# Raw projection tiles as fillers, finished at the merge, and first tiles multiplied as the input arrives

## The chip, the cores and the metric

One core of a Trainium2 chip runs the whole layer. The metric is the device time of one execution in microseconds, as a median of several runs. The engines are named as the profile names them: PE (TensorE, matmuls), PEld (its weight loads), DVE (VectorE), ACT (ScalarE), POOL (GpSimd) and SP (SyncE, which issues all DMAs of this kernel).

## The reference

A decoder layer over 1024 positions of width 1024. One projection of the normalized input feeds three mixers in parallel; their outputs are gated, merged and followed by a feed-forward part:

```python
proj = rmsnorm(x, g_mix) @ w_in
y_fox = forgetting_attention(fq, fk, fv, fox_f, ...)        # 8 heads of 64
y_sc = sb * causal_dwconv(sc * sv, sc_conv_w)               # 3 taps
dn_qkv = silu(causal_dwconv(dn_qkv, dn_conv_w))             # 4 taps
o_dn = gated_delta_rule(l2norm(dq), l2norm(dk_), dv_, g, beta)
y_dn = rmsnorm(o_dn, dn_norm_gain) * silu(z)
gates = sigmoid(br_gate)                                    # 3 x 1024 channels
merged = sum((ys @ w_branch) * gates)                       # over the 3 branches
x = x + merged @ w_o
x = x + (silu(u_gate) * u_val) @ w_down                     # u = dwconv3(rmsnorm(x) @ w_up)
x = x + sigmoid(rmsnorm(x, g_ple) @ w_ple_gate) * (p @ w_ple)
```

## The kernel before

Everything lies with channels on the 128 partitions and positions along the free axis. Each float32 operand is split into a high and a low float32r part, and a product takes three matmuls (high times high, high times low, low times high). A "tile" of the projection is 128 output channels: `dense` (line 151) makes it in two halves of 512 positions, each 8 input blocks times 3 matmuls into one PSUM bank, 48 matmuls in all, and hands each half to an evacuation function. `wload` (147) loads the 512 KB of weights and `wsplit` (139) splits them: ACT copies the high part, and POOL (in the merge and later DVE, line 949) subtracts to get the low part. The projection's operand is the unnormalized x; the factor 1/rms per position (`rs`) comes in as a product at each evacuation.

The input is read in `first_norm` (321): per block of 128 channels a DMA, the split into high and low (`norm_operand`, lines 267 and 268), squares on ACT and their sums (`sumsq`, line 277) on DVE for one half and on POOL for the other; 32 narrow matmuls for the few scalar logits stand after that, and `make_rstd` (280) gives `rs`. One tile, the first attention q, has its weights loaded early. `scalars` (383) works out decays and cumulative sums in a long series of small DVE instructions.

Then come three stages. The attention (lines 898 to 922) runs 8 heads in 4 blocks each (`softmax`, `weigh`), with q, k and v tiles of head pairs (`fox_proj`, 506). The solve (`dn_solve`, 720) inverts 32 triangular blocks: it builds the matrices (715, 731), transposes them on DVE (737), runs a substitution of 31 steps on DVE (743, 745), and joins blocks by small matmuls. The recursion (lines 932 to 946) steps a state through 8 chunks. All are chains on DVE and ACT, and between them `filler` (887) puts independent projection tiles by the table `PLAN` (31): letters k, v, q are DeltaNet tiles (`dn_tile`, 693: scaling at line 700, four taps at 470 and 472, silu at 666 to 674), s a tile of the short convolution (`short_conv`, 476: C, v and B of a channel block in turn), z an output gate (`z_tile`, 685), g a branch gate (`gate_tile`, 677). Each evacuation finishes its tile: scale, convolve, sigmoid, store. A filler may not be issued before a mark some steps back. The order on every engine is set by the framework's planner from simulated times, in program order of priority. During these stages two PSUM banks (`mm`) serve the tiles.

The merge (lines 958 to 1046) first makes the gate tiles that are left, 17 of 24, with six banks; then it multiplies each branch's output with its weights and the stored gates, in the order short convolution, attention, DeltaNet (its z product on POOL, line 984), and goes through w_o. The feed-forward stages follow and are not touched.

Of the kernel before, what the change touches and what calls it, by code (L numbers as in the profile page):

```python
# [7 lines left out]
F32 = mybir.dt.float32  # L8
# [40 lines left out]
def hybrid_block(ctx: ExitStack, tc: tile.TileContext, I, out, dbg=None):  # L49
# [254 lines left out]
    zdr = dr.tile([P, 4, T], F32, tag="zdr", name="zdr")  # L304
# [14 lines left out]
    early = {}  # L319

    def first_norm():
# [10 lines left out]
        xr, xg = [pt("xr", 8, T) for _ in range(KT)], []  # L332
# [9 lines left out]
        few = [smb(), smb()]  # L342
        for nb in range(2):
            for kt in range(KT):
                h, l = xg[kt]
                for n, x in ((32, h), (16, l)) if kt == 0 else ((16, l), (32, h)):
                    mm(few[nb][:n], wsp[:, kt * 32 : kt * 32 + n], x[:, NB[nb]], kt == 0 and n == 32,
                       kt == KT - 1 and n == 32)
        for kt in range(KT):
            sumsq(acc, xr[kt], kt == 0, (V, G))  # L350
        return xg, make_rstd(acc), few
# [124 lines left out]
    def short_conv(j):  # L476
        hold = {}

        def ev_sc(nb, ps):
            t = pt("sc", 3)  # L480
            V.tensor_tensor(out=t, in0=ps, in1=rs[:, NB[nb]], op=ALU.mult)
            hold["c", nb] = t

        def ev_sv(nb, ps):
            cv = conv_in(nb, hold.get(("cv", 0)), 3)
            hold["cv", nb] = cv
            t = cv[:, 2:514]
            V.tensor_tensor(out=t, in0=ps, in1=rs[:, NB[nb]], op=ALU.mult)
            G.tensor_tensor(out=t, in0=t, in1=hold["c", nb], op=ALU.mult)
            o = conv_out(cv, C_SC + 3 * j, 3)  # L490
            y = hold["c", nb]
            G.tensor_tensor(out=y, in0=o, in1=rs[:, NB[nb]], op=ALU.mult)
            hold["y", nb] = y

        def ev_sb(nb, ps):
            y = hold["y", nb]
            V.tensor_tensor(out=y, in0=ps, in1=y, op=ALU.mult)
            Q.dma_start(ydr[1][j][:, NB[nb]], y)

        def run(kind):  # L500
            u, f = {"c": (U_SC, ev_sc), "v": (U_SV, ev_sv), "b": (U_SB, ev_sb)}[kind]
            dense(wload(I["win"][u + j]), KT, xg, f)
        return run


    def fox_proj(j):
# [42 lines left out]
        def run(kind):  # L549
# [5 lines left out]
            dense(early.pop(u + j, None) or wload(I["win"][u + j]), KT, xg, f)  # L555
# [121 lines left out]
    def gate_tile(b, dt):  # L677
        def f(nb, ps):
            g = tmp("o")
            V.tensor_tensor(out=g, in0=ps, in1=rs[:, NB[nb]], op=ALU.mult)  # L680
            Q.dma_start(gdr[b, dt][:, NB[nb]], sigmoid(g))
        gdr[b, dt] = dr.tile([P, T], F32, tag=f"g{b}{dt}", name=f"g{b}{dt}")
        dense(wload(I["win"][U_GT + 8 * b + dt]), KT, xg, f)

    def z_tile(h):
        def f(nb, ps):
            z = tmp("o")
            V.tensor_tensor(out=z, in0=ps, in1=rs[:, NB[nb]], op=ALU.mult)
            silu(z)
            Q.dma_start(zdr[:, h, NB[nb]], z)  # L690
        dense(wload(I["win"][U_Z + h]), KT, xg, f)

# [27 lines left out]
    def dn_solve():  # L720
        A, TT = (pt(n, 1, 4096).rearrange("p (x j) -> p x j", j=P) for n in ("A", "TT"))
        G.memset(TT, 0.0)
# [517 lines left out]
```

## Time and profile before

| | us |
| --- | --- |
| median of 3 runs | 2048.36 (2048.19 to 2049.76) |
| the profiled execution | 2044.89 |
| span from its first to its last instruction | 2043.1 |

The profile is of one execution. Its page gives busy times of each engine and the costliest groups of instructions, and the trace can be asked for stretches, timelines, and who waited for whom. PE is the busiest engine. A busy time of PE says that matmuls were in flight, not at which rate; the rate is seen by their number in a stretch. The granted clock is a share of 2.4 GHz, and 0.5 of it is the lower level, 1.2 GHz. Idle time is put down to the instruction that ended it.

### The profile page before, as it was taken

What the parts mean: (1) busy time and instruction counts of PE and PEld (TensorE: products, weight loads), DVE (VectorE), ACT (ScalarE), POOL (GpSimd) and SP (SyncE); (2) the same over time, 40 slices, a digit from 0 to 9 for tenths busy, and PEclk for the clock granted to TensorE, in tenths of its full rate; (3) what the DMA queues carried; (4) which work ended last, traced back from release to release, by engine and by line L of the source; (5) the groups of instructions that cost most, each with busy time, mean ns of one, the idle gap of its engine ahead of it and who ended that gap; (6) DMA issues with size and microseconds to landing.
All of it is one profiled execution on the core that took longest, in us unless ns stands there. A gap on an engine that the chain in (4) does not pass through costs nothing. (4 is left out here: it accounts for less than half of the span.)

```text
span 2043.1 us, 25369 instructions
## 1 busy us (share of the span) xinstructions
PE 1959.1 (96%) x9281; PEld 1617.9 (79%) x9281; DVE 1368.0 (67%) x2190; ACT 903.1 (44%) x1639; POOL 575.5 (28%) x457
## 2 busy tenths in 40 slices
PE   6899999998987999999999999999999999999998
PEld 4788888887766888888888888777777777888887
DVE  7887888797999354222264636978787878544564
ACT  6566777765334334322221325544444444212351
POOL 4455335333444221000015310334343341000210
PEclk8999999999988999999999999999999999999999
DMA  3122121123311333522274523111222216432132
GB/s 147 56 73 77 45 69 55 61 69 88 106 70 49 108 105 92 191 98 103 95 273 154 184 99 134 62 52 64 91 83 73 92 63 227 144 93 73 52 108 89
DMA packets 96877, 202.63 MB, mean 99 GB/s; under 512 B 8720, under 2 KB 39792, under 8 KB 96752
## 3 DMA queue, kind: packets, MB, share of 16 engines
q1 hardware_dynamic: 96752, 201.01, 29.3%
q8 instruction: 73, 1.20, 0.2%
q14 instruction: 52, 0.43, 0.1%
HBM read 150.59 MB, written 50.38 MB: 98 GB/s over the span
## 5 line engine op out<-in xcount | busy, mean ns | idle before, releaser
L126 PE MATMUL mm<-xg,wo 128*128 128x512 f32 x6224 | 1508.5, 395 | 41.0 <-DVE cv L700 18.8
L126 PEld LDWEIGHTS mm<-xg,wo 128*128 128x128 f32 x6224 | 1166.8, 189 | 295.6 <-DVE wo L130 18.3
L126 PE MATMUL mm<-a,wo 128*128 128x512 f32 x1216 | 303.3, 389 | 0.0
L129 ACT ACTIVATE wo<-wr 128x512 fp32r<-128x512 f32 x232 | 144.6, 627 | 310.2 <-PE mm L126 301.9
L126 PEld LDWEIGHTS mm<-a,wo 128*128 128x128 f32 x1216 | 228.4, 188 | 47.9 <-ACT u L224 0.4
L130 POOL TENSOR_TENSOR wo<-wr,wo 128x512 fp32r<-128x512 f32 x94 | 131.6, 1405 | 173.0 <-ACT wo L129 149.7
L130 DVE TENSOR_TENSOR wo<-wr,wo 128x512 fp32r<-128x512 f32 x138 | 109.6, 794 | 61.6 <-ACT wo L129 60.8
L1141 DVE TENSOR_TENSOR a<-mm,a 128x512 f32<-128x512 f32 x96 | 65.2, 687 | 92.1 <-PE mm L126 92.0
L277 POOL TENSOR_TENSOR tmp<-tmp,tmp 128x512 f32<-128x512 f32 x21 | 27.7, 1324 | 286.9 <-ACT tmp L275 284.9
L472 DVE SCALAR_TENSOR_TENSOR o<-cv,cols,o 128x512 f32<-128x512 f32 x88 | 86.1, 984 | 6.2 <-ACT o L470 5.4
L970 DVE TENSOR_TENSOR tmp<-mm,rs 128x512 f32<-128x512 f32 x34 | 23.5, 691 | 91.2 <-PE mm L126 91.2
L130 DVE TENSOR_TENSOR wo<-wq,wo 128x512 fp32r<-128x512 f32 x68 | 79.1, 1165 | 2.9 <-ACT wo L129 2.7
L1054 DVE SCALAR_TENSOR_TENSOR o<-cw,cols,o 128x1024 f32<-128x1024 f32 x44 | 77.7, 1767 | 0.0
L984 POOL TENSOR_TENSOR yr<-yr,yr 128x1024 f32<-128x1024 f32 x4 | 9.6, 2397 | 240.6 <-DVE xg L130 211.8
L129 ACT ACTIVATE wo<-ws 128x512 fp32r<-128x512 f32 x80 | 50.2, 630 | 56.5 <-PE mm L126 56.4
L594 ACT ACTIVATE pp<-pp,small 128x512 f32<-128x512 f32 (+2 forms) x96 | 58.3, 610 | 28.7 <-DVE small L588 28.4
L674 POOL TENSOR_TENSOR o<-o,sg 128x512 f32<-128x512 f32 x32 | 46.5, 1453 | 74.1 <-ACT sg L669 64.9
L1086 POOL TENSOR_TENSOR cg<-o,cg 128x1024 f32<-128x1024 f32 x22 | 55.5, 2523 | 40.7 <-ACT cg L1085 40.7
L196 POOL TENSOR_TENSOR ws<-wq 128x512 f32<-128x512 f32 x20 | 29.3, 1466 | 109.8 <-DMA wq<-wup 109.8
L1002 POOL TENSOR_TENSOR a<-a,sg 128x512 f32<-128x512 f32 x32 | 50.6, 1584 | 32.4 <-DVE sg L1001 32.4
L196 POOL TENSOR_TENSOR ws<-wq,wq 128x512 f32<-128x512 f32 x20 | 43.7, 2184 | 56.3 <-DVE wo L130 52.3
L1052 ACT ACTIVATE o<-cw,cols 128x1024 f32<-128x1024 f32 x22 | 25.4, 1157 | 75.3 <-DVE cw L220 75.3
(287 smaller groups left out, 2496.1 us busy)
## 6 DMA issues: line engine op xcount, KB each, us to landing
wr<-win SPq DMA_DIRECT2D x64, 512.0 KB, 3.5
wq<-wup SPq DMA_DIRECT2D x44, 512.0 KB, 3.6
sg<-g SPq DMA_DIRECT2D x48, 256.0 KB, 3.1
ad<-o SPq DMA_DIRECT2D x20, 512.0 KB, 3.8
wq<-ad SPq DMA_DIRECT2D x20, 512.0 KB, 4.6
wr<-wdn SPq DMA_DIRECT2D x20, 512.0 KB, 3.7
g<-tmp SPq DMA_DIRECT2D x34, 256.0 KB, 2.0
wr<-wbr SPq DMA_DIRECT2D x12, 512.0 KB, 3.6
```

Of the source, the lines that this page charges most:

```text
L126: pe[0] = nc.tensor.matmul(o, lhsT=l, rhs=r, start=start, stop=stop, skip_group_check=more)
L129: S.activation(h, x, AF.Copy)
L130: (eng or V).tensor_tensor(out=l, in0=x, in1=h.bitcast(F32), op=ALU.subtract)
L196: (G if e == "g" else V).tensor_tensor(out=o, in0=x, in1=y, op=op)
L277: eng[nb].tensor_tensor(out=acc[nb], in0=acc[nb], in1=sq, op=ALU.add)
L472: V.scalar_tensor_tensor(out=o, in0=cv[:, i : i + 512], scalar=col(c0 + i), in1=o, op0=ALU.mult, op1=ALU.add)
L594: S.activation(t[:, :w], t[:, :w], AF.Exp, bias=mn[:, k - 1 : k], scale=-1.0, accum_out=sm[:, i : i + 1])
L674: G.tensor_tensor(out=o, in0=o, in1=sg, op=ALU.mult)
L1002: G.tensor_tensor(out=m, in0=m, in1=t, op=ALU.add)
L1054: V.scalar_tensor_tensor(out=o, in0=cv[:, i : i + T], scalar=col(c0 + i), in1=o, op0=ALU.mult, op1=ALU.add)
L1086: G.tensor_tensor(out=sg, in0=o, in1=sg, op=ALU.mult)
L1141: V.tensor_tensor(out=x2[dt][:, NB[nb]], in0=ps, in1=x2[dt][:, NB[nb]], op=ALU.add)
```

## The change

Fillers of the kinds s, z and g become one kind, r: a raw tile, copied out of its bank by ACT and stored unscaled (24 of them: 12 of the short convolution, 4 output gates, 8 branch gates). What their evacuations did (scale by rs, convolve, sigmoid, multiply) is done at the merge, one item after each of the 16 gate tiles that are left there, on DVE and ACT from loaded raw tiles. The DeltaNet tiles all move ahead of the solve; the solve has eight raw tiles, the recursion's first six steps the last nine. In `first_norm` each arriving block is at once multiplied for the scalar logits, for the first q tile and for one raw tile (in banks of its own, five of `sm` where there were four); the sums of squares and these two tiles' weight splits are all on DVE. q and k of the first heads come ahead of `scalars`. The branches are merged in the order 0, 1, 2, the zeroing of TT is cut in eight, and one evacuation takes another buffer.

```diff
-PLAN = {"start": "kgs", "tail": "", "solve": "zzzzzvvvv",
-        "steps": ["zs", "sz", "zs", "s", "s", "ks", "g", "sgs", "gs"],
-        "fox": [["", "", "", "s"],
-                ["k", "gs", "", ""],
-                ["", "", "", ""],
+PLAN = {"start": "krr", "tail": "", "solve": "rrrrrrrr",
+        "steps": ["rr", "rr", "rr", "r", "r", "r", "r", "r", "r"],
+        "fox": [["", "", "", "v"],
+                ["k", "v", "", ""],
+                ["", "", "", "r"],
                 ["", "v", "", ""],
-                ["ks", "", "k", "k"],
-                ["", "", "g", ""],
-                ["", "", "", "s"],
-                ["v", "s", "g", ""]]}
+                ["kr", "", "q", "v"],
+                ["", "", "q", "r"],
+                ["", "", "", "q"],
+                ["k", "q", "r", ""]]}
...
         for kt in range(KT):
             Q.dma_start(xr[kt], I["xT"][kt])
             xg.append(norm_operand(kt, xr[kt], C_G1))
-            if kt == 1:
-                early[U_FQ] = wload(I["win"][U_FQ])
+            if kt == 0:
+                wq = wload(I["win"][U_FQ], eng=V)
+            if kt == 2:
+                wr, _, _, evac = raw_tile(spare["r"].pop(0), V)
+            if kt:
+                sumsq(acc, xr[kt - 1], kt == 1, (V, V))
+        sumsq(acc, xr[KT - 1], False, (V, V))
+        for kt in range(KT):
+            for nb in range(2):
+                h, l = xg[kt]
...
+            for w, ps in ((wq, pq), (wr, pr_)):
+                for nb in range(2):
+                    step(ps[nb], w, kt, xg[kt], nb, kt == 0, kt == KT - 1)
+        for nb in range(2):
+            evac(nb, pr_[nb])
...
+    def raw_tile(u, eng=None):
+
+        raw[u] = dr.tile([P, T], F32, tag=f"r{u}", name=f"r{u}")
+
+        def f(nb, ps):
+            o = tmp("o")
+            S.activation(o, ps, AF.Copy)
+            Q.dma_start(raw[u][:, NB[nb]], o)
+        return wload(I["win"][u], eng=eng), KT, xg, f
...
+            def short_conv(j):
+                c, v, cv = load(raw[U_SC + j]), load(raw[U_SV + j]), yr(T + 2)
+                V.memset(cv[:, 0:2], 0.0)
+                t = cv[:, 2 : T + 2]
+                mul(t, c, v)
+                mul(t, t, rs)
+                mul(t, t, rs)
+                S.activation(c, cv[:, 0:T], AF.Copy, scale=col(C_SC + 3 * j))
+                for i in (1, 2):
+                    V.scalar_tensor_tensor(out=c, in0=cv[:, i : i + T], scalar=col(C_SC + 3 * j + i), in1=c,
+                                           op0=ALU.mult, op1=ALU.add)
+                b = load(raw[U_SB + j])
+                mul(c, c, b)
+                mul(c, c, rs)
+                Q.dma_start(ydr[1][j], c)
+
+            def dn_gated(j):
+                z, y, sg = load(raw[U_Z + j]), load(ydn[:, j, :]), yr()
+                mul(z, z, rs)
+                S.activation(sg, z, AF.Sigmoid)
+                mul(z, z, sg)
+                mul(y, y, z)
+                Q.dma_start(ydr[2][j], y)
+
+            def gate(b, dt, nb, ps):
+                g = tmp()
+                if ps is None:
+                    Q.dma_start(g, raw[U_GT + 8 * b + dt][:, NB[nb]])
+                mul(g, g if ps is None else ps, rs[:, NB[nb]])
+                S.activation(g, g, AF.Sigmoid)
+                Q.dma_start(gdr[b, dt][:, NB[nb]], g)
...
+                    if u not in raw:
+                        dense(wload(I["win"][u]), KT, xg, lambda nb, ps, b=b, dt=dt: gate(b, dt, nb, ps))
+                        if rest:
+                            rest.pop(0)()
```

## Rows read from the trace of the kernel before

**Rows 1.** The page, part 1: busy time, share of the span and number of instructions of each engine.

```profile
PE 1959.1 (96%) x9281; PEld 1617.9 (79%) x9281; DVE 1368.0 (67%) x2190; ACT 903.1 (44%) x1639; POOL 575.5 (28%) x457
```

**Rows 2.** The stretches view, 50 us each: length, then busy time and number of instructions of PE, PEld, DVE, ACT and POOL, the granted TensorE clock as a share of 2.4 GHz, the busy share of the DMA engines and GB/s.

```profile
0.00:50.00 50.00, 33.87 (x119) 20.84 (x120) 36.55 (x42) 29.91 (x52) 23.63 (x21) 0.86 0.40 150
50.00:100.00 50.00, 44.66 (x191) 35.83 (x189) 44.03 (x85) 28.17 (x51) 21.11 (x17) 0.93 0.16 54
...
450.00:500.00 50.00, 43.29 (x234) 36.38 (x233) 35.83 (x95) 26.38 (x61) 13.41 (x14) 0.93 0.24 72
500.00:550.00 50.00, 47.33 (x237) 39.07 (x235) 44.80 (x101) 21.41 (x36) 21.11 (x16) 1.00 0.48 138
550.00:600.00 50.00, 40.28 (x153) 31.41 (x154) 49.69 (x61) 17.40 (x29) 21.41 (x17) 0.90 0.17 61
600.00:650.00 50.00, 38.62 (x201) 32.23 (x199) 48.57 (x72) 19.20 (x33) 22.21 (x20) 0.90 0.15 53
650.00:700.00 50.00, 44.91 (x363) 40.42 (x362) 23.16 (x40) 16.98 (x37) 14.22 (x11) 0.97 0.34 96
...
850.00:900.00 50.00, 50.00 (x222) 41.42 (x221) 11.66 (x17) 11.12 (x18) 0.00 (x0) 1.00 0.38 134
...
1700.00:1750.00 50.00, 49.26 (x216) 40.03 (x215) 40.03 (x50) 18.90 (x24) 3.40 (x2) 1.00 0.79 285
```

**Rows 3.** The same view of three longer stretches: the attention, the triangular solve, and the recursion.

```profile
100.00:470.00 370.00, 364.75 (x1893) 306.04 (x1894) 307.69 (x720) 265.25 (x561) 163.73 (x136) 1.00 0.20 65
...
490.00:650.00 160.00, 136.24 (x634) 111.04 (x633) 147.37 (x243) 59.02 (x99) 65.49 (x55) 0.94 0.28 86
...
675.00:850.00 175.00, 171.19 (x1012) 149.44 (x1012) 78.41 (x198) 69.19 (x174) 36.90 (x32) 1.00 0.40 123
```

**Rows 4.** Timelines of the first 100 us, of PE, then DVE, ACT and POOL: start, duration (both us), engine, line, operation, output<-input, how many in a row, and in brackets the idle time before the first with what ended it.

```profile
6.76 2.10 PE L126 MATMUL sm<-xg,wsp 128*32 128x512 f32 x4 [6.76 <-ACT xg L267]
...
11.49 1.59 PE L126 MATMUL mm<-xg,wo 128*128 128x512 f32 x4
...
14.48 2.92 PE L126 MATMUL mm<-xg,wo 128*128 128x512 f32 x12
...
72.40 8.11 PE L126 MATMUL mm<-xg,wo 128*128 128x512 f32 x24 [4.49 <-DVE o L540]
...
6.74 1.41 DVE L268 SCALAR_TENSOR_TENSOR xg<-xr,cols,xg 128x512 fp32r<-128x512 f32 x2 [2.91 <-ACT xg L267]
...
12.31 3.33 DVE L268 SCALAR_TENSOR_TENSOR xg<-xr,cols,xg 128x512 fp32r<-128x512 f32 x2 [1.29 <-ACT xg L267]
15.57 3.50 DVE L277 TENSOR_TENSOR acc<-acc,tmp 128x512 f32<-128x512 f32 x2
...
31.68 1.48 DVE L277 TENSOR_TENSOR acc<-acc,tmp 128x512 f32<-128x512 f32 x2
...
35.00 2.73 DVE L268 SCALAR_TENSOR_TENSOR xg<-xr,cols,xg 128x512 fp32r<-128x512 f32 x4
...
40.86 0.69 DVE L261 SCALAR_TENSOR_TENSOR rs<-tmp,y 128x512 f32<-128x512 f32 x1
...
5.98 1.33 ACT L267 ACTIVATE xg<-xr,cols 128x512 fp32r<-128x512 f32 x2 [2.48 <-DMA xr<-xT]
...
12.12 2.98 POOL L130 TENSOR_TENSOR wo<-wr,wo 128x512 fp32r<-128x512 f32 x2
15.06 10.22 POOL L277 TENSOR_TENSOR acc<-acc,tmp 128x512 f32<-128x512 f32 x6
```

**Rows 5.** Groups of instructions in the solve, 490 to 650 us, first of DVE, then of POOL: line, engine, operation, output<-input, shapes, how many | busy us, mean ns of one | idle us before them and what ended it.

```profile
L472 DVE SCALAR_TENSOR_TENSOR o<-cv,cols,o 128x512 f32<-128x512 f32 x33 | 35.1, 1072 | 0.8 <-ACT o L470 0.8
L743 DVE TENSOR_TENSOR pr<-TL,LA 128x1 f32<-128x1 f32 (+30 forms) x31 | 30.9, 997 | 0.5
...
L666 DVE TENSOR_SCALAR sg<-o 128x512 f32<-128x512 f32 x18 | 7.6, 422 | 0.3
L700 DVE TENSOR_TENSOR cv<-mm,rs 128x512 f32<-128x512 f32 x11 | 7.5, 678 | 0.0
L688 DVE TENSOR_TENSOR o<-mm,rs 128x512 f32<-128x512 f32 x8 | 5.5, 682 | 0.1
...
L674 POOL TENSOR_TENSOR o<-o,sg 128x512 f32<-128x512 f32 x18 | 27.2, 1515 | 45.2 <-ACT sg L669 44.0 <-DVE X L773 1.2
```

**Rows 6.** The view of who waited for whom in 540 to 650 us: us in total, times, longest; one row.

```profile
PE mm L126 <- DVE cv L700: 18.8, 6, 7.8
```

**Rows 7.** Groups of the whole span, as in rows 5: what one operation of a kind takes.

```profile
L130 POOL TENSOR_TENSOR wo<-wr,wo 128x512 fp32r<-128x512 f32 x94 | 131.6, 1405 | 173.0 <-ACT wo L129 149.7 <-DMA gb<-cdr 11.0 <-DVE pr L743 3.4
L130 DVE TENSOR_TENSOR wo<-wr,wo 128x512 fp32r<-128x512 f32 x138 | 109.6, 794 | 61.6 <-ACT wo L129 60.8
...
L130 DVE TENSOR_TENSOR xg<-yr,xg 128x1024 fp32r<-128x1024 f32 x14 | 17.4, 1250 | 5.4 <-ACT xg L129 5.4
...
L210 ACT ACTIVATE u<-mm 128x512 f32<-128x512 f32 x20 | 11.9, 593 | 0.0
```

**Rows 8.** The DMA issues (output<-input, queue, operation, number, KB each, median us from issue to landing), and the view of who waited, for SyncE's queue.

```profile
yr<-y SPq DMA_DIRECT2D x8, 512.0 KB, 4.9
...
SPq L136 <- DVE wo L130: 315.5, 64, 12.4
```

More of the change, by code (lines that the diff above doesn't have):

```diff
@@ L149, in wload, with step @@
         return [wsplit(wr[:, c : min(c + 512, n)], eng or weng[0]) for c in range(0, n, 512)]
+    def step(ps, w, j, x, nb, first, last):
+        h, l = x
+        wh, wl = w[j // 4]
+        sl = slice(j % 4 * P, j % 4 * P + P)
+        mm(ps, wh[:, sl], h[:, NB[nb]], first, False)
+        mm(ps, wh[:, sl], l[:, NB[nb]], False, False)
+        mm(ps, wl[:, sl], h[:, NB[nb]], False, last)
     def dense(w, kts, mov, evac, koff=0):
@@ L316, in hybrid_block @@
     U_r = const([P, P], F32R, "U_r")
-    early = {}
+    early, xg = {}, []
+    spare = {"r": [*range(U_SB, U_DN), *range(U_Z, U_GT)] + [U_GT + 8 * b + dt for b in (2, 0) for dt in (7, 6, 5, 4)]}
     def first_norm():
@@ L331, in first_norm @@
         acc = [pt("acc", 2) for _ in range(2)]
-        xr, xg = [pt("xr", 8, T) for _ in range(KT)], []
+        xr = [pt("xr", 8, T) for _ in range(KT)]
+        few, pq, pr_ = ([bank(r) for _ in range(2)] for r in ("sm", "mm", "sm"))
         for kt in range(KT):
@@ L341, in first_norm @@
         V.tensor_copy(U_r, Uf)
[L342 to L351, printed above, removed]
+        early[U_FQ] = pq
+        return make_rstd(acc), few
     def exp32(x):
@@ L474, in conv_out @@
         return o
[L476 to L503, printed above, removed]
+    raw = {}
+    def raw_tile(u, eng=None):
[5 more added lines that the diff above has]
+        return wload(I["win"][u], eng=eng), KT, xg, f
     def fox_proj(j):
@@ L554, in run @@
             u, f = {"q": (U_FQ, evac_qk(True)), "k": (U_FK, evac_qk(False)), "v": (U_FV, evac_v)}[kind]
-            dense(early.pop(u + j, None) or wload(I["win"][u + j]), KT, xg, f)
+            if u + j in early:
+                for nb, ps in enumerate(early.pop(u + j)):
+                    f(nb, ps)
+            else:
+                dense(wload(I["win"][u + j]), KT, xg, f)
         return run, (qs, kh, kl, vs)
@@ L675, in silu @@
         return sg
[L677 to L691, printed above, removed]
     def dn_tile(kind, h):
@@ L721, in dn_solve @@
         A, TT = (pt(n, 1, 4096).rearrange("p (x j) -> p x j", j=P) for n in ("A", "TT"))
-        G.memset(TT, 0.0)
+        for c in range(8):
+            G.memset(TT[:, 4 * c : 4 * c + 4, :], 0.0)
         for c in range(8):
@@ L924, in hybrid_block @@
         with phase("f2", psum=dict(sm=SM2, po=1), X=8, et=2):
-            filler("kkkk")
             mark()
@@ L930, in hybrid_block @@
                 filler(PLAN["solve"], 1)
-                filler("vvvvqqqq", 1)
             with phase("f2t"):
@@ L945, in hybrid_block @@
                     filler(PLAN["steps"][c], 1)
-                filler("zzzz" + "s" * 12, 0)
+                filler("r" * len(spare["r"]), 0)
     weng[0] = V
@@ L958, in hybrid_block, with yr, mul, load @@
         with phase("me", tmp=9, sg=4, yr=4):
-            def yr():
-                return pt("yr", 4, T)
-            for b in (1, 0, 2):
+            def yr(w=T):
+                return pt("yr", 4, T + 4)[:, 0:w]
+            def mul(o, x, y):
+                V.tensor_tensor(out=o, in0=x, in1=y, op=ALU.mult)
+            def load(d):
+                t = yr()
+                Q.dma_start(t, d)
+                return t
+            def short_conv(j):
[13 more added lines that the diff above has]
+                Q.dma_start(ydr[1][j], c)
@@ L963, in hybrid_block @@
+            rest = [lambda f=f, j=j: f(j) for f in (short_conv, dn_gated) for j in range(4)]
+            for b in range(3):
                 for dt in range(8):
-                    if (b, dt) in gdr:
-                        continue
                     gdr[b, dt] = dr.tile([P, T], F32, tag=f"g{b}{dt}", name=f"g{b}{dt}")
-                    def ev_g(nb, ps, b=b, dt=dt):
-                        g = tmp()
-                        V.tensor_tensor(out=g, in0=ps, in1=rs[:, NB[nb]], op=ALU.mult)
-                        S.activation(g, g, AF.Sigmoid)
-                        Q.dma_start(gdr[b, dt][:, NB[nb]], g)
@@ L973, in hybrid_block @@
-                    dense(wload(I["win"][U_GT + 8 * b + dt]), KT, xg, ev_g)
+                    if U_GT + 8 * b + dt in raw:
+                        rest.append(lambda b=b, dt=dt: [gate(b, dt, nb, None) for nb in range(2)])
+            for b in range(3):
+                for dt in range(8):
+                    u = U_GT + 8 * b + dt
+                    if u not in raw:
+                        dense(wload(I["win"][u]), KT, xg, lambda nb, ps, b=b, dt=dt: gate(b, dt, nb, ps))
+                        if rest:
+                            rest.pop(0)()
@@ L975, in hybrid_block @@
+            for f in rest:
+                f()
             merged = [big() for _ in range(8)]
-            for bi, b in enumerate((1, 0, 2)):
+            for b in range(3):
                 ys = []
                 for j in range(4):
-                    y, h, l = yr(), xgt(), xgt()
-                    Q.dma_start(y, ydr[b][j] if b < 2 else ydn[:, j, :])
-                    if b == 2:
-                        zr = yr()
-                        Q.dma_start(zr, zdr[:, j, :])
-                        G.tensor_tensor(out=y, in0=y, in1=zr, op=ALU.mult)
+                    y, h, l = load(ydr[b][j]), xgt(), xgt()
```

38 lines of the change are left out of this document (16 added, 22 removed).

## Prediction

> **What bounds the kernel now.** I read the busy times first: PE holds 96% of the span, so time can only come from the 4% in which it idles, from stretches at the lower clock, or from fewer matmuls [rows 1]. The edit removes no matmul: every tile keeps its 48. So the second view is the 50 us stretches, to see where PE is not full [rows 2]. At 850 us a full stretch holds 222 matmuls, or 225 ns each, and a tile of 48 costs 10.8 us. I price each stretch as its idle time plus (1 - granted clock) x 50 us, since 1.2 GHz does half the work of 2.4 (a ceiling, as half speed costs nothing while PE idles). That gives 16.1 + 7.0 = 23.1 us lost at 0 to 50, 5.3 + 3.5 = 8.8 at 50 to 100, and then, from 450 to 700, 10.2 + 2.7 + 14.7 + 16.4 + 6.6 = 50.6. The attention between them idles only 370 - 364.8 = 5.2 us, the recursion 3.8 [rows 3], and the merge at 850 nothing. So some 91 us can be won, in two places.
>
> Third I read what PE waits for there. In the solve DVE is busy 147.4 of 160 us while ACT and POOL are not half full [rows 3]; PE waits for the DVE instruction that empties a projection's bank, 18.8 us in six waits [rows 6]. DVE runs the substitution (line 743) among 35.1 + 7.6 + 7.5 + 5.5 = 55.7 us of convolution, sigmoid and scaling for the filler tiles [rows 5]. At the start PE has its first operand at 6.76 us and then waits again and again for the next [rows 4].
>
> **The start.** The new loop does the 32 small matmuls, 96 of two tiles and 4 of the norm before rs is known: 132 x 225 ns = 29.7 us. From 6.8 us, with the first 6 or so at half speed (four matmuls took 1.59 us at 11.5, twelve 2.92 at 14.5 [rows 4]), that is 3 more: PE ends near 39.5. Can the operands keep up? DVE needs 8 pairs of line 268 at 1.41, 7 pairs of sums at 1.48, and 4 weight halves at 0.79 [rows 4, 7]: 11.3 + 10.4 + 3.2 = 24.9 us from 6.74, so 31.6. ACT's eight pairs at 1.33 and its squares and splits (20 x 0.6, the price of a copy [rows 7]) end at 5.98 + 10.6 + 12 = 28.6. Both lie ahead of PE. rs stood ready for its first half at 41.5 before (40.86 + 0.69) [rows 4]. Its chain (four ACT operations of 0.6 us, three of DVE of 0.69, two matmuls) is some 5 us a half; from 31.6 it ends at 37 and 41, about when PE runs out. So at about 41 us PE has one tile more behind it than before: 10.8 us and a little, I take 12. Ends: 0, if rs comes a tile later and PE waits for it, and 16.
>
> This rests on the pairs at 1.41 and 1.48 us. The same pairs took 3.33 and 3.50 while POOL split weights and added squares, from 12.1 to 25.3 us [rows 4]; the change gives both jobs to DVE, and POOL is nearly idle. The Trainium skill, SBUF — State Buffer, section Who interferes with whom, says that a DVE instruction with two SBUF inputs contends with a GpSimd instruction that reads SBUF, and that the one that comes second blocks for the whole of the first. By that rule the moved work costs DVE nothing, since DVE stood still meanwhile; by a plain count of its instructions DVE gets 8 us more to do. The rows side with the rule.
>
> Q and k are now projected ahead of the scalar chain, whose place in DVE's queue cost PE 4.49 us before the matmul at 72.4, in a stretch with a clock of 0.93 [rows 2, 4]. The v tile's evacuation still stands behind that chain, so I take 2, of 0 to 8.
>
> **The attention.** It and its start ran 16 tiles; now 18, and a nineteenth at the start. That moves work and adds none for PE. For DVE: six more convolved v and q tiles, at 2 x (0.68 + 3 x 1.07 + 0.42) = 8.6 us each by the dear rows of the solve [rows 5], 52 us; six short-convolution tiles go, two channel blocks of 2 x (3 x 0.68 + 2 x 1.07) = 8.4, 17 us, and four gates of 2 x 1.1, 9 us: 26 more over two tiles' 21.6 us. DVE's share goes from 307.7/370 = 83% to 334/392 = 85% [rows 3]; POOL and ACT stay below it. No engine overtakes PE, but half-tiles may wait. I take a loss of 5 us; ends 0 and 58 (second rival).
>
> **The solve.** It keeps 8 fillers, of 10, all raw: weights split on ACT and POOL, bank emptied by an ACT copy of 0.59 us [rows 7], nothing on DVE. The 55.7 us leave DVE, and with them POOL's 27.2 us of silu products beside it [rows 5]; the substitution stays. From 490 to 675 was 185 us; I take 50 off, for the rest lay in waits that PE's part will now show: 135. PE's work in it is 384 x 0.225 = 86.4 for the fillers, and some 37 for its own small matmuls (185 less the 40.4 lost from 500 to 700 and the ten fillers' 108): 123. So 12 us idle, 4 at half speed, and the 10.2 at the attention's end as now: 26 lost in place of 50.6, 24.6 won. Ends: chain 145 (14 won) and chain 124 (36).
>
> **Recursion and merge.** Nine fillers stay in the recursion, but at the first six steps; for the last three the merge's gates must fill. PE is at 171/175 now [rows 3]; I charge 1 us, of -2 to 9. The merge has one tile fewer and takes the finishing: four short convolutions (five products of 1.25 us and two taps of about the same [rows 7], 35 us), four output gates (15), eight gates (16 x 0.69, 11), besides its own 32 evacuations and 32 splits at about 0.7 (45): DVE 106 of 16 x 10.8 = 173 us. Its DMAs (20 loads and 8 stores of 512 KB, 16 and 16 of 256 KB, and the dense tiles' 17 MB: 40 MB) are 230 GB/s, where one stretch moved 285 at a share of 0.79 [rows 2]. Six banks hold three tiles' results. I charge 1 us, of 0 to 39 (third rival). The POOL product at the merge that goes was hidden under a full PE: 0.
>
> **Sum** on the profiled execution: 2044.9 - 12 - 2 + 5 - 24.6 + 1 + 1 = 2013.3. The median of the runs shown lies 3.5 above that execution, so **2017 us**.
>
> **Rivals.**
> - POOL is not the reason. If the start's pairs of 3.4 us were slow for another cause than POOL's work beside them, DVE's 31 us there grow by 7 sums and 4 halves, 8.4 us; the last operand comes at 46, and of the 12 us about 2.4 stay: 2027. For it: nothing but that POOL and the weight loads ran at the same time. Against: alone, from 31.7 us on, the same forms ran at 0.7.
> - Slower: PE waits for evacuations in the attention as it did in the solve. Twelve more convolved half-tiles with the solve's 18.8/6 = 3.1 us each [rows 6], and 1.7 each for the clock that fell there (0.10 of 100 us, over six waits [rows 2]): 58 us in place of 5, 2070. It outweighs the gain from 3 us a half-tile. For it: DVE at 83% already, two banks only. Against: in the solve it stood at 98% between 550 and 650; here the planner has other matmuls to put between.
> - Slower: the finishing's loads block SyncE's queue. Its tiles have four buffers, one short convolution takes all, and the next item's loads wait in front of the weights' loads. Eight items at the 4.9 us of a landing are 39 us, if they reach PE: 2056. Against: weights are fetched well ahead now (SyncE waited up to 12.4 us for a buffer with PE full [rows 8]); it decides only where a block passes one tile's 10.8 us.
> - No gain: the solve's chain does not shrink, because POOL's splits still lengthen the substitution (a step of 997 ns on average [rows 5]) and two fillers fewer leave PE idle. A chain of 165 loses 165 - 123 + 10 + 5 = 57, 7 more than now; with the start's 14 and 7 of charges the sum is 2044.9 - 14 + 7 + 7 + 3.5 = 2048. That is also the case in which the planner, whose own simulated times order the queues, does not do what the plan says.
>
> **How the numbers follow.** Forecast 0.68, its own range 1995 to 2037 (the ends above, taken in part); POOL not the reason 0.05; no gain 0.09, of which 0.01 is still faster; attention 0.11; merge 0.05; a weak gain between 2037 and 2044 0.02. From 2000 or so to 2046 holds the forecast, the 2027 case and most of no gain, and the low end is set at 1994 for a chain of 124 with a full 16 at the start: about 0.8. A measurement of this kernel can tell about 0.2%, 4 us, from no change: faster 0.76, same 0.08, slower 0.16.
>
> **What would show it.** Right: PE's idle in 0 to 50 falls below 11 us and line 268's pairs take 1.4 us throughout; no PE wait for a convolution's scaling in the solve, DVE there under 90% and the solve some 50 us shorter; ACT copies of 0.6 us into the raw tiles; 16 gate tiles at the merge with PE still at 50 of 50. Wrong: waits of 3 us on the convolution's scaling between 100 and 500 us, clock below 1 there; PE idle at the merge beside loads of the raw tiles; line 743 as slow as before.

## The result, and the profile after

The changed kernel takes 2026.93 us (median of 4 runs, 2026.01 to 2027.74), the kernel before 2048.28 beside it: a ratio of 0.990 with an interval of 0.9882 to 0.9918. The forecast was 2017. The profiled execution took 2026.68 us, its span 2024.9 against 2043.1.

Part 1 of the page, after. PE does the same 9281 matmuls in 6.4 us less busy time [rows 1]; the rest of the 18.2 us is idle time:

```profile
PE 1952.7 (96%) x9281; PEld 1615.1 (80%) x9281; DVE 1352.6 (67%) x2173; ACT 897.7 (44%) x1635; POOL 517.0 (26%) x419
```

The 50 us stretches of the changed kernel, columns as in [rows 2]:

```profile
0.00:50.00 50.00, 39.06 (x154) 27.39 (x155) 33.77 (x51) 31.09 (x54) 11.24 (x12) 0.97 0.45 171
50.00:100.00 50.00, 46.77 (x204) 36.92 (x202) 41.59 (x84) 30.17 (x53) 19.46 (x17) 0.97 0.11 37
...
500.00:550.00 50.00, 44.25 (x226) 36.22 (x226) 29.12 (x87) 19.59 (x40) 17.23 (x23) 0.93 0.50 142
550.00:600.00 50.00, 49.82 (x229) 41.29 (x228) 45.65 (x71) 10.86 (x20) 11.55 (x8) 1.00 0.29 101
600.00:650.00 50.00, 39.20 (x301) 35.41 (x300) 34.08 (x54) 11.71 (x24) 14.85 (x11) 0.90 0.11 38
650.00:700.00 50.00, 50.00 (x317) 43.25 (x317) 14.15 (x33) 17.86 (x41) 9.07 (x8) 1.00 0.44 131
...
800.00:850.00 50.00, 41.45 (x222) 35.94 (x221) 22.57 (x48) 15.52 (x48) 1.27 (x1) 0.86 0.39 144
850.00:900.00 50.00, 50.00 (x223) 41.42 (x222) 43.10 (x47) 16.24 (x24) 0.00 (x0) 1.00 0.83 280
```

The first two rows lose 12.4 and 4.7 us by the prediction's price, where they lost 23.1 and 8.8. Around the solve, 500 to 550 and 600 to 650 still lose 9.3 and 15.8, the stretch between almost nothing, and DVE is down to 29 to 46 of 50 us. New is 800 to 850: 8.6 us idle and a clock of 0.86, in the place where the recursion ends. At 850 the merge's PE is full beside 43.1 us of DVE work and 280 GB/s.

The start, timelines of PE, then DVE, then POOL of the changed kernel (columns as in [rows 4]):

```profile
37.88 0.39 PE L126 MATMUL sm<-h,ones_r 128*128 128x512 f32 x1
...
39.77 0.49 PE L126 MATMUL sm<-h,ones_r 128*128 128x512 f32 x1 [1.26 <-ACT h L289]
...
43.74 0.43 PE L388 MATMUL sm<-cst,sm 32*128 32x32 f32 x4 [2.09 <-DVE sm L385]
...
6.45 1.42 DVE L271 SCALAR_TENSOR_TENSOR xg<-xr,cols,xg 128x512 fp32r<-128x512 f32 x2 [2.64 <-ACT xg L270]
...
25.84 3.49 DVE L271 SCALAR_TENSOR_TENSOR xg<-xr,cols,xg 128x512 fp32r<-128x512 f32 x2
...
42.28 0.69 DVE L264 SCALAR_TENSOR_TENSOR rs<-tmp,y 128x512 f32<-128x512 f32 x1
...
45.11 0.84 DVE L264 SCALAR_TENSOR_TENSOR rs<-tmp,y 128x512 f32<-128x512 f32 x1
...
24.19 6.30 POOL L130 TENSOR_TENSOR wo<-wr,wo 128x512 fp32r<-128x512 f32 x3 [23.36 <-ACT wo L129]
```

Line 268 of before is 271 here. Its pairs take 1.41 us where [rows 4] had 3.33; the one exception, 3.49, lies inside POOL's three splits from 24.19. But `rs` (line 264) comes at 43.0 and 46.0, not at 37 and 41. The matmuls with ones_r, which sum the squares over the partitions, stand in PE's queue behind the two tiles' last matmuls: the first comes at 37.88, the second half's at 39.77 after a wait of 1.26, and the logits' first (L388), which need `rs`, after 2.09 more. On ACT the second half's operand (L289) came only at 39.10, behind a weight split that had waited 8.58 us for PE, until 36.72, and behind the raw tile's copies at 37.40.

Groups of the solve, 500 to 640 us, one each of DVE, ACT and POOL (columns as in [rows 5]):

```profile
L727 DVE TENSOR_TENSOR pr<-TL,LA 128x1 f32<-128x1 f32 (+30 forms) x31 | 27.7, 893 | 1.1
...
L496 ACT ACTIVATE o<-mm 128x512 f32<-128x512 f32 x17 | 10.2, 599 | 46.3 <-PE mm L126 26.4 <-issue 17.0 <-DMA gb<-cdr 2.7
...
L130 POOL TENSOR_TENSOR wo<-wr,wo 128x512 fp32r<-128x512 f32 x17 | 24.1, 1418 | 67.2 <-ACT wo L129 67.2
```

No convolution, sigmoid or scaling is left on DVE. The raw tiles are ACT copies of 0.6 us (L496). The substitution's 31 products (line 727 here, then 743 of before: shortest, median and longest in ns, first and last start in us, shapes):

```profile
L727 DVE TENSOR_TENSOR pr<-TL,LA x31: 160/771/1961, 563.2 to 605.5; 128x1 f32<-128x1 f32 x1, 128x4 f32<-128x4 f32 x1, 128x9 f32<-128x9 f32 x1, 128x16 f32<-128x16 f32 x1
L743 DVE TENSOR_TENSOR pr<-TL,LA x31: 150/1041/2370, 538.1 to 608.7; 128x1 f32<-128x1 f32 x1, 128x4 f32<-128x4 f32 x1, 128x9 f32<-128x9 f32 x1, 128x16 f32<-128x16 f32 x1
```

From first to last start it is 42.3 us for 70.6. One product takes 893 ns on average against 997, 3 us over all 31. Between 538 and 609 us of before, 31.8 us of the fillers' convolution, scaling and sigmoid stood on DVE among them. So the chain shrank by 28 us mostly because nothing stands between its instructions any more, and little because each became faster.

PE in the solve, around the first joining matmul (`sm<-X,A`):

```profile
584.75 25.32 PE L126 MATMUL mm<-xg,wo 128*128 128x512 f32 x111
620.87 2.08 PE L126 MATMUL sm<-X,A 128*128 128x128 f32 x8 [10.79 <-DVE X L741]
622.60 4.50 PE L126 MATMUL mm<-xg,wo 128*128 128x512 f32 x15
```

PE idles 10.8 us and then does eight matmuls of 128x128 in 2.08 us (granted clock 0.50 from 620.87 to 622.60), which takes 1.06 at the full clock (from 627.82 us on). Yet 15 filler matmuls come directly behind: the fillers were not all used when it stood still.

PE at the end of the recursion:

```profile
814.66 0.63 PE L855 MATMUL po<-cst,on 128*128 128x128 f32 x4 [3.23 <-DVE small L848]
...
819.27 0.64 PE L126 MATMUL po<-vn,pd 128*128 128x128 f32 x2
823.75 1.09 PE L855 MATMUL po<-cst,on 128*128 128x128 f32 x4 [3.85 <-DVE yr L952]
824.49 15.82 PE L126 MATMUL mm<-xg,wo 128*128 128x512 f32 x59
```

The waits of 3.2 and 3.9 us stand bare, the eight matmul pairs between them run at half speed (granted clock 0.50 from 816.1 to 820.0), and the merge's first tile follows the recursion's last transposition (L855) by 0.74 us. It did so before as well, by 0.38:

```profile
836.33 0.63 PE L871 MATMUL po<-cst,on 128*128 128x128 f32 x4 [1.49 <-DVE on L868]
836.71 13.64 PE L126 MATMUL mm<-xg,wo 128*128 128x512 f32 x59
```

### The profile page after: what moved, and what is told of

Read it like the earlier page. It is cut to its first block, busy times and chain, and to the rows that moved or that the text cites. A ratio compares the mean times of both kernels' runs of the same rounds, so it can differ in the third digit from the quotient of the medians.

```text
span 2024.9 us, 25492 instructions
## 1 busy us (share of the span) xinstructions
PE 1952.7 (96%) x9281; PEld 1615.1 (80%) x9281; DVE 1352.6 (67%) x2173; ACT 897.7 (44%) x1635; POOL 517.0 (26%) x419
## 5 line engine op out<-in xcount | busy, mean ns | idle before, releaser
L126 PE MATMUL mm<-xg,wo 128*128 128x512 f32 x6176 | 1492.4, 393 | 18.3 <-DVE wo L130 13.2
L484 DVE SCALAR_TENSOR_TENSOR o<-cv,cols,o 128x512 f32<-128x512 f32 x72 | 73.3, 1018 | 10.0 <-ACT o L482 9.2
L496 ACT ACTIVATE o<-mm 128x512 f32<-128x512 f32 x46 | 27.4, 595 | 90.7 <-PE mm L126 70.7
L1070 ACT ACTIVATE o<-cw,cols 128x1024 f32<-128x1024 f32 x22 | 25.4, 1156 | 77.1 <-DVE cw L223 77.1
L199 DVE TENSOR_TENSOR ws<-ws,wq 128x512 f32<-128x512 f32 x20 | 14.9, 745 | 66.5 <-POOL ws L199 66.5
L130 DVE TENSOR_TENSOR pl<-pq,ph 128x512 fp32r<-128x512 f32 (+1 forms) x80 | 49.6, 629 | 14.4 <-ACT ph L129 14.2
L979 ACT ACTIVATE tmp<-tmp 128x512 f32<-128x512 f32 x48 | 30.1, 630 | 65.4 <-DVE tmp L943 60.2
```

The lines of the kernel that those rows point to most:

```text
L126: pe[0] = nc.tensor.matmul(o, lhsT=l, rhs=r, start=start, stop=stop, skip_group_check=more)
L130: (eng or V).tensor_tensor(out=l, in0=x, in1=h.bitcast(F32), op=ALU.subtract)
L199: (G if e == "g" else V).tensor_tensor(out=o, in0=x, in1=y, op=op)
L484: V.scalar_tensor_tensor(out=o, in0=cv[:, i : i + 512], scalar=col(c0 + i), in1=o, op0=ALU.mult, op1=ALU.add)
L979: S.activation(g, g, AF.Sigmoid)
```

## The experiments

Each kernel is the changed one with the edit shown. Ratios are against runs of the kernel before on the same chip; the changed kernel's own is 0.990. The medians of the kernel before beside these kernels lie between 2045.1 and 2048.3, so times of two kernels compare to some 3 us only, and the difference by the ratios stands beside where it is another. The table holds, for each, the loss by the prediction's price, summed over the 50 us stretches (views of stretches; in the kernel before each stage up to the merge lies up to 27 us from its place after).

| kernel | us | 0 to 100 | 100 to 500 | 500 to 850 | 850 to 1200 | 1200 to 1700 |
| --- | --- | --- | --- | --- | --- | --- |
| before | 2048.3 | 32.0 | 15.2 | 41.9 | 0.0 | 14.9 |
| after | 2026.9 | 17.2 | 9.6 | 40.8 | 0.0 | 18.4 |
| steps spread (e1) | 2019.0 | 18.7 | 9.6 | 34.6 | 0.0 | 18.2 |
| ninth tile (e2) | 2035.4 | 18.3 | 15.5 | 43.2 | 0.0 | 17.9 |
| finished tiles back in the solve (e4) | 2053.4 | 17.0 | 7.5 | 86.2 | 4.4 | 14.9 |
| POOL at the start (e5) | 2035.5 | 24.3 | 10.6 | 41.2 | 0.0 | 17.3 |
| one tile at the start (e6) | 2019.9 | 18.5 | 6.0 | 39.5 | 0.0 | 16.1 |
| early root (e8c) | 2025.6 | 12.6 | 14.9 | 40.3 | 0.0 | 16.5 |
| scalars first (e9) | 2028.5 | 18.1 | 10.0 | 41.8 | 0.0 | 15.2 |
| order, eight tiles | 2017.5 | 18.3 | 10.0 | 28.4 | 0.0 | 16.1 |
| order, nine tiles | 2011.9 | 18.7 | 10.0 | 21.9 | 0.0 | 15.5 |
| two in the first step (e11) | 2020.0 | 18.2 | 10.1 | 36.5 | 0.0 | 15.7 |
| order and one tile (e12) | 2006.2 | 19.9 | 5.7 | 17.2 | 0.0 | 18.8 |

The feed-forward column moves by up to 4 us between kernels that do not touch that stage; differences of this size in the sum are not read.

**The recursion's tiles, spread (e1).**

```diff
-        "steps": ["rr", "rr", "rr", "r", "r", "r", "r", "r", "r"],
+        "steps": ["r", "r", "r", "r", "r", "r", "r", "r", "r"],
```

> Only the recursion's fillers move: one raw tile at each of the nine steps, where the changed kernel has 2,2,2,1,1,1 and none at the last three. Theory: the 8.6 us that PE idles and the 13.7 us at 1.2 GHz between 800 and 850 us are there because nothing is left to put into the last steps; then some 9 us come back, about 2018 (2015 to 2021), with PE at 50 of 50 and a clock of 1.00 in that stretch. Rival: the loss belongs to the way into the merge (its first tile starts only after the recursion's last transpose, whatever runs before); then the idle stays behind the last transpose, the time stays at 2025 to 2028.

2018.98 us (2015.89 to 2022.9), ratio 0.9865, interval 0.9848 to 0.9881: 8 us below the changed kernel, 7 by the ratios. Its stretches, from the execution of 2022.9:

```profile
600.00:650.00 50.00, 39.20 (x278) 34.87 (x276) 35.45 (x55) 10.50 (x21) 14.80 (x11) 0.86 0.12 43
650.00:700.00 50.00, 47.55 (x332) 41.46 (x331) 14.73 (x35) 16.42 (x40) 7.57 (x6) 1.00 0.45 129
700.00:750.00 50.00, 48.26 (x290) 42.90 (x289) 18.69 (x61) 18.77 (x55) 9.01 (x7) 0.97 0.34 109
...
800.00:850.00 50.00, 50.00 (x248) 42.04 (x247) 24.30 (x40) 17.24 (x41) 1.29 (x1) 1.00 0.57 200
```

From 800 to 850 PE is full at a clock of 1.00, where the changed kernel lost 15.6 us. Part is given back: 600 to 750 loses 23.5 (10.8, 2.45 and 1.74 idle, and 0.14 and 0.03 of 50 us for the clock) for 15.8. So tiles for the recursion's end are worth 7 to 8 us net, and the gates of the merge don't take their place.

**Two tiles in the first step, none in the last (e11).**

```diff
-        "steps": ["rr", "rr", "rr", "r", "r", "r", "r", "r", "r"],
+        "steps": ["rr", "r", "r", "r", "r", "r", "r", "r", ""],
```

> The recursion's fillers as 2,1,1,1,1,1,1,1,0. In the spread run (2019.0) the last steps were full, but the first ones, from 650 to 725 us, lost some 7 us more than with two tiles each. Theory: the two chunks' preparation ahead of the first step wants the second tile, so most of the 7 us come back and the bare last step costs 3 to 5: 2015 to 2019. Rival: nine tiles are one too few for nine steps plus the preparation, and every bare place costs the same: 2019 to 2021.

2020.0 us (2016.43 to 2024.62), ratio 0.9864, interval 0.9843 to 0.9886: the rival's number, though the runs cover the theory's too. 650 to 800 is full, and 800 to 850 loses 4.3 idle and 0.07 of clock, 7.8 together. What a tile early saves, a bare last step costs.

**A ninth tile in the solve (e2).**

```diff
-PLAN = {"start": "krr", "tail": "", "solve": "rrrrrrrr",
+PLAN = {"start": "kr", "tail": "", "solve": "rrrrrrrrr",
```

> One raw tile goes from the start of the attention to the solve, which then has nine. Theory: the changed solve is bound by its own chain on DVE (about 135 us) and runs out of fillers 11 us before PE gets its next matrix; a ninth tile of 10.8 us fits in for nothing, the idle of 10.8 us at 610 us and the 10 us at 1.2 GHz behind it vanish, and the attention is a tile shorter: about 2012 (2009 to 2017). Rival: the tile delays the chain, since its weight splits on POOL stand against DVE and its matmuls stand in PE's queue ahead of the chain's; then it only changes places, 2025 to 2030.

A miss: 2035.38 us (2034.24 to 2036.2), ratio 0.995, interval 0.9935 to 0.9964. PE around the first joining matmul:

```profile
617.02 2.08 PE L126 MATMUL sm<-X,A 128*128 128x128 f32 x8 [10.68 <-DVE X L741]
618.75 7.77 PE L126 MATMUL mm<-xg,wo 128*128 128x512 f32 x25
```

The idle time is still 10.7 us. The tile went behind the joining matmuls, where 63 filler matmuls now stand, and the attention, from which it was taken, loses 15.5 for 9.6. So the wait is not mended by more tiles alone: they were there, but the queue's order put them late. The fillers are programmed behind `dn_solve`, so the joining matmuls have the higher priority; the next two kernels test that.

**The order, with nine tiles and with eight.** The fillers are programmed inside `dn_solve`, ahead of the joining loop, and the steps hold the rest:

```diff
-    def dn_solve():
+    def dn_solve(fill):
...
+        fill()
         for k in range(11):
...
-                Xs = dn_solve()
+                Xs = dn_solve(lambda: filler(PLAN["solve"], 0))
                 mark()
-                filler(PLAN["solve"], 1)
```

> The solve's fillers stand in the program ahead of the joining of the blocks instead of behind it, so that all of them come first in PE's queue; there are nine, the ninth taken from the recursion's last step, whose others have one each (as in the spread run, 2019.0). Theory: PE idles 10.8 us before the first joining matmul because the planner put that matmul after 369 filler matmuls, whatever their number (369 too with nine tiles), taking the substitution for shorter than it is; with 432 ahead PE is busy up to some 626 us, the wait is under 2 us, the clock stays at 1.00, and the recursion's bare last step costs up to 5: 2006 to 2013. Rival: the chain behind the substitution is what counts, and what it had inside (fillers between its steps) is idle time now: 2017 to 2023.

2011.86 us (2009.37 to 2017.6), ratio 0.9831, interval 0.9813 to 0.9848.

```profile
584.82 42.55 PE L126 MATMUL mm<-xg,wo 128*128 128x512 f32 x187
627.20 1.05 PE L126 MATMUL sm<-X,A 128*128 128x128 f32 x8
```

No idle time, and the eight matmuls take 1.05 us: the clock stayed up. With eight tiles:

> The ordering alone: the fillers programmed ahead of the joining matmuls, but eight tiles as in the changed kernel, and one tile in each of the recursion's nine places. If the order is what counts, all 384 filler matmuls come ahead of the first joining one in place of 369; those 15 are 3.4 us of the 10.8 that PE stood idle there, and the rest of the idle time and its half speed stay: 2015 to 2018, beside 2019.0 with the recursion spread alone. If the ninth tile is what counts, it is no better than that, 2018 to 2020. If both are needed only in part, it falls to 2012 to 2014, as with nine.

2017.47 us (2016.93 to 2021.25), ratio 0.9863, interval 0.9848 to 0.9878.

```profile
584.81 32.57 PE L126 MATMUL mm<-xg,wo 128*128 128x512 f32 x143
625.06 2.07 PE L126 MATMUL sm<-X,A 128*128 128x128 f32 x8 [7.67 <-DVE X L741]
```

The 15 matmuls moved ahead cut the idle time by 3.1 us, to 7.67 (15 x 0.225 is 3.4), and the half speed stays. Eight tiles are 7.7 us too few, and a ninth helps only ahead of the joining matmuls: it needs both. The loss from 500 to 850 goes 34.6 (e1), 28.4, 21.9. In time the order alone can't be told from none (0.9863 for the 0.9865 of e1); with the ninth tile it is 0.9831.

**Finished tiles back in the solve (e4).** The eight DeltaNet v and q tiles go into the solve, eight raw ones into the attention:

```diff
-PLAN = {"start": "krr", "tail": "", "solve": "rrrrrrrr",
-        "fox": [["", "", "", "v"],
+PLAN = {"start": "krr", "tail": "", "solve": "vvvvqqqq",
+        "fox": [["", "", "", "r"],
...
```

> The eight v and q tiles and eight raw tiles change places: v and q in the solve, raw tiles in the attention. All else is the changed kernel. Theory: what won the 25 us in the solve is that nothing of its fillers runs on DVE; with the convolutions back, PE waits for them again there (18.8 us in six waits before), the clock falls, and the solve is some 40 us longer than now while the attention gains a few: about 2047 (2040 to 2055). Rival: the gain is from less DVE work ahead of the merge altogether, wherever it stands; then 2025 to 2032.

2053.43 us (2051.04 to 2056.07), ratio 1.0039, interval 1.0024 to 1.0054: the whole gain gone and more. The view of who waited, 600 to 660 us (total, times, longest), and PE's timeline:

```profile
PE sm L126 <- DVE X L741: 35.0, 1, 35.0
```

```profile
649.44 2.07 PE L126 MATMUL sm<-X,A 128*128 128x128 f32 x8 [35.00 <-DVE X L741]
...
658.20 1.09 PE L126 MATMUL sm<-X,A 128*128 128x128 f32 x8
```

The substitution runs from 551.6 to 634.0 us, 82 us for 42, and PE stands still for 35 us. The time is the expected one, the wait only in part: PE waits for a convolution's scaling 9.1 us in all from 490 to 665, and the rest is the one wait for the substitution. The 86.2 of the table overstates, since the price counts the low clock in idle time too (0.54 in these 35 us). The attention loses 2 us less (7.5 for 9.6). So which kind of tile stands where is worth some 27 us (28 by the ratios), and nearly all of it lies in the solve. (Before, six of these tiles stood there, here eight.) This is the core of the change.

**One half of the sums, and the splits, back on POOL (e5).**

```diff
-                wq = wload(I["win"][U_FQ], eng=V)
+                wq = wload(I["win"][U_FQ], eng=G)
...
-                sumsq(acc, xr[kt - 1], kt == 1, (V, V))
+                sumsq(acc, xr[kt - 1], kt == 1, (V, G))
```

> Only the start: one half of the sums of squares and the first two tiles' weight splits go back to POOL. Theory: POOL's work lengthens DVE's two-input instructions beside it; the pairs of the operand's low part, 1.41 us now, take 3.3 to 3.5 again, the last operand comes 5 to 8 us later, and the first 50 us lose so much: 2031 to 2035. Rival: the pairs were slow for another cause (the loads of x and weights that land at that time); then they stay at 1.4, DVE has 8 us less to do, and the time is 2022 to 2027.

2035.53 us (2033.77 to 2037.76), ratio 0.9951, interval 0.9937 to 0.9966: 8.6 us of the gain is lost, 10 by the ratios. Timelines of PE, then DVE:

```profile
47.89 0.49 PE L126 MATMUL sm<-h,ones_r 128*128 128x512 f32 x1 [1.26 <-ACT h L289]
...
12.07 1.78 DVE L280 TENSOR_TENSOR acc<-acc,tmp 128x512 f32<-128x512 f32 x1
13.78 3.49 DVE L271 SCALAR_TENSOR_TENSOR xg<-xr,cols,xg 128x512 fp32r<-128x512 f32 x2
...
25.70 1.40 DVE L271 SCALAR_TENSOR_TENSOR xg<-xr,cols,xg 128x512 fp32r<-128x512 f32 x2
...
29.97 1.32 DVE L361 CAST U_r<-cst 128x128 fp32r<-128x128 f32 x1
```

DVE has less to do and is later: a pair of line 271 takes 3.49 us while POOL works and 1.40 when it pauses, an addition 1.78 (0.64 each in the changed kernel, whose pairs of additions take 1.28). The ones_r matmul that waited last comes at 47.89 for 39.77. These rows agree with the rule that the prediction cited, of the Trainium skill, SBUF — State Buffer, section Who interferes with whom, by which a DVE instruction with two SBUF inputs contends with a GpSimd instruction that reads SBUF.

**One tile in the arrival loop (e6).** The raw tile of the loop becomes an ordinary filler behind it:

```diff
-            for w, ps in ((wq, pq), (wr, pr_)):
+            for w, ps in ((wq, pq),):
...
-PLAN = {"start": "krr", "tail": "", "solve": "rrrrrrrr",
+PLAN = {"start": "krrr", "tail": "", "solve": "rrrrrrrr",
```

> The arrival loop multiplies only the q tile; the raw tile goes to the fillers at the start of the attention. Sums and splits stay on DVE. Theory of the prediction: while the input arrives and rs is not known, PE has room for a second tile of 10.8 us that needs no rs; without it PE waits for rs instead, the first 50 us idle some 8 to 10 us longer: 2034 to 2038. Rival: what won the start is the quicker operands alone (POOL off, blocks in order), and the second tile only moved: 2025 to 2029, idle in the first 50 us as now (10.9 us).

The second miss: 2019.87 us (2019.22 to 2022.2), ratio 0.9868, interval 0.9853 to 0.9883. Without the second tile it is 7 us faster. PE, then DVE:

```profile
36.87 0.44 PE L384 MATMUL sm<-cst,sm 32*128 32x32 f32 x4 [1.70 <-DVE sm L381]
37.47 5.04 PE L126 MATMUL mm<-xg,wo 128*128 128x512 f32 x21 [0.16 <-DVE o L506]
...
35.34 0.69 DVE L264 SCALAR_TENSOR_TENSOR rs<-tmp,y 128x512 f32<-128x512 f32 x1
...
38.17 0.91 DVE L264 SCALAR_TENSOR_TENSOR rs<-tmp,y 128x512 f32<-128x512 f32 x1
```

`rs` comes at 36.0 and 39.1 us, 7 earlier than in the changed kernel, and from 37.47 to 50 PE works through. Two of its stretches:

```profile
0.00:50.00 50.00, 36.67 (x145) 23.90 (x146) 39.27 (x62) 34.42 (x61) 14.09 (x15) 1.00 0.40 150
...
100.00:500.00 400.00, 394.02 (x2032) 329.67 (x2031) 330.32 (x756) 285.35 (x599) 178.03 (x149) 1.00 0.20 70
```

At the start PE idles 13.3 us where it idled 10.9; with a full clock the first 100 us lose 18.5 for 17.2. The attention loses 6.0 for 9.6 (2032 matmuls for 2001 in the same 400 us), with one more free tile in it. The second tile filled 1.3 us and was missing where it would have filled 3.6. The table puts the other parts of the 7 us at 1.3 (500 to 850) and 2.3 (feed-forward, not explained).

**The root ahead of the last block's matmuls (e8c).** Both tiles stay, but the sums' matmuls are programmed earlier:

```diff
         for kt in range(KT):
+            if kt == KT - 1:
+                rs1 = make_rstd(acc)
...
-        return make_rstd(acc), few
+        return rs1, few
```

> One call moves: the sums of the norm over channels (four matmuls and the chain to rs) stand ahead of the last input block's matmuls in the program, no longer behind them. Theory: of the start's 14 us the changed kernel won 11, since rs comes at 43 and 46 us, not at 37 and 41: its first matmul stands behind 16 others in PE's queue, up to 37.9 us. With the first half's pair ahead of these, rs's first half comes some 3 us earlier and the 4.4 us that PE idles between 38 and 44 us shrink to 1 or 2: 2023 to 2025. Rival: rs waits for ACT (which stands still for a weight buffer until 36.7 us) and the sums, not for PE: 2026 to 2028, idle as now.

2025.63 us (2023.58 to 2026.32), ratio 0.9892, interval 0.9878 to 0.9907, not to be told from the changed kernel.

```profile
0.00:50.00 50.00, 42.98 (x179) 30.83 (x180) 36.37 (x60) 33.43 (x59) 13.01 (x13) 1.00 0.45 171
...
100.00:500.00 400.00, 388.13 (x1980) 323.14 (x1978) 334.03 (x748) 284.27 (x597) 174.17 (x148) 0.99 0.20 67
```

The start gains 4.6 us (7.0 idle, clock 1.00), and the attention gives them back: 11.9 idle and 0.99 in 400 us, 14.9 over its eight stretches for 9.6. What is done sooner at the start comes back here as idle time in the attention.

**The scalar chain ahead of q and k again (e9).**

```diff
-            for k in "qk":
-                proj[0][0](k)
             scalars(smt)
+            for k in "qk":
+                proj[0][0](k)
```

> The changed kernel with one part undone: the scalar chain is programmed ahead of the projections of q and k again. By the prediction's term (2 us, of 0 to 8) it takes 2029, of 2027 to 2031, with the loss between 50 and 100 us some 2 higher. Rival: the fall of the loss between 50 and 100 us from 8.8 to 4.7 came from this part entire, and it takes 2031 or more. Second rival: the planner finds the same order from its own times, and nothing moves: within 1 of the changed kernel.

2028.48 us (2026.92 to 2028.67), ratio 0.9911, interval 0.9898 to 0.9925. That is 1.6 us above the changed kernel, 2 by the ratios, as the prediction's 2 us say, but the intervals overlap widely: it can't be told from nothing. The loss from 50 to 100 did not rise (4.0 for 4.7), so if the gain is there, it isn't where the prediction saw it.

**Both at once (e12).** The order with nine tiles, and one tile in the loop ("start" is "krrr").

> This joins the two edits that beat the changed kernel most: nine tiles put ahead of the joining matmuls in the solve (2011.9 alone, about 15 below the changed kernel) and one tile in place of two in the loop over the arriving input (2019.9 alone, 7 below). Theory: they act in different stages, so they add: 2005, of 2002 to 2009, with PE never idle for over 1 us ahead of the first joining matmul and the reciprocal root in two halves before 40 us. Rival: what the one tile gave was that the tile left over covered the attention's last gaps, and the second edit already takes the same tiles: then nothing is added and it stays at 2010 to 2013.

2006.23 us (2005.95 to 2006.46), ratio 0.9804, interval 0.9791 to 0.9817: faster than both kernels, by 41 us (2047.6 on this chip) and some 20. PE in the solve:

```profile
584.71 36.20 PE L126 MATMUL mm<-xg,wo 128*128 128x512 f32 x159
620.75 1.05 PE L126 MATMUL sm<-X,A 128*128 128x128 f32 x8
```

Within the noise the two edits add (14 and 7 by the ratios). Of what is left, 19.9 us lie in the start and 17.2 from 500 to 850.

## Why the prediction was right, and what was mis-sized

The sign and the two places were right; the time came out 10 us above the forecast. Its terms against the stretches:

| term | predicted | lost before | lost after | measured |
| --- | --- | --- | --- | --- |
| start and q, k (0 to 100) | -14 | 32.0 | 17.2 | -14.8 |
| attention | +5 | 5.0 | 9.6 | +4.6 |
| its end and the solve | -24.6 | 50.6 | 25.2 | -25.4 |
| recursion | +1 | 1.5 | 15.5 | +14.0 |
| merge | +1 | 0 | 0 | 0 |

Before: 0 to 100, 100 to 450, 450 to 700, 700 to 850 and 850 to 1200 ([rows 2] and the table of the experiments). After: 0 to 100, 100 to 500, 500 to 700, 700 to 850 and 850 to 1200. The prediction's 3.8 for the recursion [rows 3] began at 675, where its 50.6 for the solve ends at 700, so it had counted 2.3 us twice. The sum is -21.6 for the -31.6 of the prediction. The feed-forward, which the prediction left out, lost 2.8 more (18.4 for 14.9 and, from 1700 to 1750, 0.7 [rows 2]): -18.8, beside -18.2 in the spans. The medians fell by 21.4, since the traced execution of before lay 3.4 below its median and that of after lies at it.

**The recursion** is the mis-sized term, and it alone makes up more than the miss (13.0 of 10 us; the other terms came out 3.0 better than predicted). "For the last three the merge's gates must fill" does not happen, before or after: they follow the last transposition. The prediction had charged 1 and put the bound at 9, and the 14.0 lie outside it. The traces of before could have shown it: there too the first gate came 0.4 us behind the recursion's last transposition. What holds the gates back is not shown. e1, which undoes this part alone, won 7 to 8.

**The solve** was right in size, and in its main reason: the DVE work for the fillers held up the substitution (e4: 35 us of waiting comes back with it). From the first product of its matrices to the last joining matmul it took 129 us (527.1 to 656.2) for 175 before, 46 off for the 50 taken. What would be left was given as 12 us idle because the fillers run out, and 10.8 came. That reason is right for 7.7 of them; 3.1 are matmuls that the queue's order holds back, and the same order keeps a ninth tile from helping (e2, and the order with eight and nine).

**The start** had the right sum by luck, with a part that is wrong. POOL is the reason the operands were late (e5: 8.6 us of time), so the first rival is out. But the second tile is not worth its 10.8 us. "rs at 37 and 41" failed: with two tiles it came at 43.0 and 46.0, since the sums' matmuls stand behind the tiles' (on ACT, too, the second half's operand came at 39.10, behind a split that waited for PE and behind the raw tile's copies), and the tile is taken from stages that needed it (e6, e8c). A tile moved is worth the gap it fills less the gap it leaves. What won the 4.1 us from 50 to 100 stays open, since putting the scalar chain back did not cost them (e9).

**Attention and merge** were as charged: no PE wait on a convolution's scaling between 100 and 500 us (the longest PE wait there on one DVE instruction is 1.2 us), and the merge's 16 finishing items hidden under a full PE. Neither of the two slower rivals showed. "No gain" would have needed the substitution to stay long; it fell from 70.6 to 42.3 us.

## What to carry to other kernels

Put fillers that need no work on the engine of a chain beside that chain, and finish them where the other engines stand idle under a full PE; count the value of a filler as the gap that it fills less the gap that it leaves. Before a wait is put down to too few fillers, look at what PE does directly after it: fillers there say that the order has its part. Here more of them did not help until it was changed, and the changed order hardly helped without more of them. And when fillers are taken from the end of a stage, see in the trace of before whether the next stage's work ever started ahead of that end.

## What the runs showed of the hardware

A cast of 128x128 on DVE, with one input only, took 1.32 us beside POOL's splits (e5, at 29.97; the splits run from 28.23 to 32.43) and 0.22 us without it in the changed kernel (at 21.90): not only instructions with two inputs are held up. After the 35 us of standing still in e4, PE's matmuls ran at half speed from 649.4 to 658.2 us, 8.8 us (granted clock 0.50), with one more wait of 1.4 us among them; after the 10.8 us in the changed kernel PE was at full speed at the latest 6.1 us after its return (0.71 from 620.87 to 626.9, then 1.00).
